# A decoder layer in split fp32: one weight block of the down projection's seven products comes by accumulating transfers alone, product 1 moves one quad forward, and the second pass takes a fourth quad in sevens

## The chip, the cores and the metric

The kernel runs on one core of a Trainium2 chip. The metric is the device time of one execution in microseconds. A trace of one profiled execution of the kernel before is at hand; times in it count from the start of the span.

## The reference

One decoder layer on 256 tokens of 2048 channels, all in fp32: a half-step SwiGLU feed-forward block, a mixer of two attention branches, and a second half-step feed-forward block, each with a residual and a layer norm. What the change touches is the last matrix product of the two feed-forward blocks, from 5632 hidden channels to 2048:

```python
def _swiglu(x, w_gate, w_up, w_down):
    return (jax.nn.silu(x @ w_gate) * (x @ w_up)) @ w_down
...
h = _layer_norm(ALPHA * h + 0.5 * _swiglu(h, ffn1_w_gate[l], ffn1_w_up[l], ffn1_w_down[l]),
                ln1_g[l], ln1_b[l])
```

## The kernel before

**Three matmuls for one.** fp32 precision is kept by splitting each operand into a rounded high part and a remainder (`split`, L154 and L155): ScalarE casts the block, VectorE subtracts the cast from it. A product of two split operands is then three matmuls, high by high, high by low, low by high (`triple`, L208 to L210). So every weight block of 128 x 1024 elements costs a cast on ScalarE and a subtraction on VectorE before TensorE can use it. The split blocks, named `wring`, stand in a ring of six pairs. A pair comes free when TensorE has used it.

**Units.** The work of a matrix product is cut into units. `unit` (L194) issues a unit's load at once, splits the weights of the unit that was loaded three units ago, and issues the matmuls of one that was prepared four units ago. So the order in which units are called sets the order on every engine, with these distances between load, split and matmuls. A list of functions due at a unit (`calls`) adds the loads of h, their splits and the like.

**The down projection.** It runs in two passes p, each over two column blocks m of 512 columns; each unit takes 256 of the 5632 rows. Four 128-row tiles of h make a quad, 11 of them. A *plain* unit multiplies one weight block with both halves b of the tokens: 2 tiles x 2 halves x 3, so 12 matmuls; a quad has four plain units per pass. A quad can also be taken *in sevens* (Strassen's scheme in Winograd's form): its four weight blocks 11, 12, 21, 22 (row pair, then column block) are combined into seven sums, each split and multiplied with one of seven forms of h, at 2 x 3 matmuls a product. The forms are made by `QuadForms.steps` from the raw h: four differences (L569) and seven split pieces, written to tiles named `xs`. Three quads, 0 to 2, go in sevens in both passes; their forms are made once, in the first pass, and kept.

**The seven products' weights** (`Sliced`, from L583). Product 1 takes block 11 as it is, 5 takes 11 + 12, 6 takes 11 + 12 + 22, 7 takes 12 + 22, 2 takes 21, 4 takes 11 + 12 + 22 + 21 and 3 takes 22; they come in the order 1, 5, 6, 7, 2, 4, 3. The sums are made in place in three buffers named `sraw`, one each for 11, 12 and 22, loaded by SyncE (L656); 21 comes into a tile of the plain units' pool `raw` of four buffers (L652). VectorE adds 12 to 11 for product 5, 22 to that for 6, 21 to that for 4 (L661). For product 7, 12 + 22 is an accumulating transfer: GpSimd issues a transfer of 22 from DRAM that is added onto the buffer of 12 (L663); only in the very first quad of the first pass VectorE adds it. A buffer is loaded anew when its last reader is done.

**Order of units.** A string, `mix`, says where a product (s) and where a plain unit (p) stands; the rest of the plain units follows. After the products' sums are complete, VectorE folds them into the residual rows `z` (L863), and after the last plain unit of a column block it adds that block and takes statistics (L880, L889). In the first feed-forward block, tables for the attention (`setup`, masks, angles) are made on VectorE and ScalarE about where the two passes meet. The h of a quad comes back from DRAM by transfers on GpSimd's queue (`get_h`, L990), called six units before its first use.

Of the kernel before, what the change touches and what calls it, by code (L numbers as in the profile page):

```python
# [11 lines left out]
F32 = mybir.dt.float32  # L12
# [47 lines left out]
def layer_kernel(ctx: ExitStack, tc: tile.TileContext, a: dict, out: bass.AP):  # L60
    nc = tc.nc
    V, S, GP, PE = nc.vector, nc.scalar, nc.gpsimd, nc.tensor
# [90 lines left out]
    def split(hi, lo, src):  # L153
        cast[0] = S.copy(hi, src)  # L154
        lows[0] = V.tensor_tensor(out=lo, in0=src, in1=hi.bitcast(F32), op=ALU.subtract)  # L155
        return lows[0]
# [426 lines left out]
    class Sliced:  # L583
# [2 lines left out]

        def __init__(self, at):
            self.at = at
            self.R = {n: act_tile([P, 1024], F32, "sraw") for n in ("11", "12", "22")}
            self.reads = {n: 0 for n in self.R}  # L590

        def run(self, w0, w1, units, forms, fold, done, calls, tail=0):

            R = self.R
            plan = {1: ("11", "11", None, "A"), 5: ("12", "11", "12", "D"), 6: ("22", "11", "22", "B"),
                    7: (None, "12", "22", "C"), 2: ("21", "21", None, (0, 0)), 4: (None, "11", "21", (0, 1)),
                    3: (None, "22", None, (1, 0))}
            uses = {"11": 4, "12": 2, "22": 3}
            banks, seen, shared = {}, {}, {}
            keys = [(n, b) for n in range(2) for b in range(2)]  # L600
            total = {key: 2 * sum(1 for u in units if len(u) == 2 and u[0] == key[0]) for key in keys}
# [36 lines left out]
            held = {}  # L638

            def product(q, p):  # L640
                load_block, src, other, key = plan[p]
                st = {}

                def by_transfer(q):
                    return tail > 0 or q > 0

                def load():
                    w = (w0, w1)[load_block[1] == "2"]
                    j = 2 * q + (load_block[0] == "2")
                    if load_block == "21":  # L650
                        held["21"] = wpool.tile([P, 1024], F32, tag="raw", name=nm("raw"), bufs=4)
                        nc.sync.dma_start(held["21"], w[j])  # L652
                    else:
                        assert self.reads[load_block] == 0, (q, p, self.reads)
                        self.reads[load_block] = uses[load_block]
                        nc.sync.dma_start(R[load_block], w[j])  # L656

                def prep():
                    t = held["21"] if src == "21" else R[src]
                    if other is not None and not (p == 7 and by_transfer(q)):  # L660
                        V.tensor_tensor(out=t, in0=t, in1=held["21"] if other == "21" else R[other], op=ALU.add)  # L661
                    if p == 5 and by_transfer(q):
                        nc.gpsimd.dma_start(R["12"], w1[2 * q + 1], accum_op=ALU.add)  # L663
                    for name in (src, other):
                        if name in R:
                            self.reads[name] -= 1
# [277 lines left out]
    def ffn(n, x, wgu, wdn, residual, g, bt, each, first=None, between=None, nxt=None, cols=None, norm=None, pending=None):  # L944
# [111 lines left out]
        spare = []  # L1056
        forms = {q: QuadForms(spare) for q in range(3)}
        down = Sliced(h_at)
        order = (1, 5, 6, 7, 2, 4, 3)

        def quad_units(quads):
            return [(m, 2 * q + i) for q in quads for m in range(2) for i in range(2)]

        for p in range(2):
            if p == 0:
                rest = deque(quad_units(range(3, KF // 4)))
                mix = "pppp" + "spspspspspspspppp" * 2 + "sp" * 7
                kept = ()
            else:
                kept = (9, 10)  # L1070
                rest = deque(quad_units((9, 10, 3, 4)) + [(m, 2 * q + i) for m in range(2) for q in (5, 6, 7, 8) for i in range(2)])
# [9 lines left out]
            for q in range(3, KF // 4):  # L1081
# [5 lines left out]
            if p == 0:  # L1087
                for q in range(3):
                    first_use = units.index((q, 1, None))
                    if q > 0:  # L1090
# [4 lines left out]
            else:  # L1095
# [528 lines left out]
```

## Time and profile before

| what | value |
|---|---|
| median of 3 runs | 1960.17 us (1960.05 to 1962.89) |
| the profiled execution's own time | 1958.59 us |
| its span, first to last instruction | 1956.8 us |
| TensorE, VectorE, ScalarE, GpSimd busy | 99%, 90%, 65%, 19% of the span |
| granted TensorE clock | 0.999 |
| down projection of the first block: first pass, mixed part of the second | 449 to 565 us, 565 to 660 us |
| the same of the second block | 1715 to 1830 us, 1830 to 1924 us |

The profile says for each engine how long it was busy, and for each idle time what ended it. An engine that is busy all the time still need not be the bound of a stretch: matmuls overlap, so a pitch, the distance of their starts, says more than a length. Idle time matters only on the engine that bounds. For the others it is a reserve, and the list of waits says what it is made of: waits for the bounding engine cost nothing, waits for a transfer may.

### The profile page before, as it was taken

What the parts mean: (1) busy time and instruction counts of PE and PEld (TensorE: products, weight loads), DVE (VectorE), ACT (ScalarE), POOL (GpSimd) and SP (SyncE); (2) the same over time, 40 slices, a digit from 0 to 9 for tenths busy, and PEclk for the clock granted to TensorE, in tenths of its full rate; (3) what the DMA queues carried; (4) which work ended last, traced back from release to release, by engine and by line L of the source; (5) the groups of instructions that cost most, each with busy time, mean ns of one, the idle gap of its engine ahead of it and who ended that gap; (6) DMA issues with size and microseconds to landing.
All of it is one profiled execution on the core that took longest, in us unless ns stands there. A gap on an engine that the chain in (4) does not pass through costs nothing.

```text
span 1956.8 us, 25750 instructions
## 1 busy us (share of the span) xinstructions
PE 1943.6 (99%) x8715; PEld 1608.7 (82%) x8715; DVE 1760.2 (90%) x2129; ACT 1277.6 (65%) x1638; POOL 376.1 (19%) x610
## 2 busy tenths in 40 slices
PE   9999999999999999999999999999999999999998
PEld 8888888888888898888888888888888888888886
DVE  7999999999898879989987777789999999999987
ACT  6677676776665566666667655566767676766652
POOL 0122212321200010102241630012221123210110
PEclk9999999999999999999999999999999999999999
DMA  9988997888878667767685798698989888888973
GB/s 319 304 241 244 269 304 238 237 267 289 291 239 258 208 221 255 238 220 257 211 256 190 234 301 279 202 294 251 251 255 283 280 232 245 272 305 259 314 246 127
DMA packets 152245, 498.30 MB, mean 255 GB/s; under 512 B 22017, under 2 KB 22321, under 8 KB 152113
## 3 DMA queue, kind: packets, MB, share of 16 engines
q1 hardware_dynamic: 110592, 371.64, 53.2%
q0 software_dynamic: 41376, 124.89, 27.1%
q8 instruction: 68, 1.11, 0.2%
q14 instruction: 65, 0.52, 0.1%
q10 hardware_dynamic: 144, 0.13, 0.0%
HBM read 466.16 MB, written 30.41 MB: 254 GB/s over the span
## 4 chain that ended last, share of the span: by engine, by line
PE 91%; DVE 5%; DMA 2%; issue 2%; ACT 0%; POOL 0%; SPq 0%; DVEq 0%; ACTq 0%
PE mm L209 25%; PE mm L208 25%; PE mm L210 25%; PE tr L209 4%; PE tr L210 4%; PE tr L208 4%; DVE wring L155 3%; DMA raw<-in_gu_dram 1%; DVE sraw L452 1%; PE tr L715 0%; DMA raw<-in_dn_dram 0%; DMA raw<-in_wgd_dram 0%; PE tr L1425 0%; PE tr L1427 0%; ACT wring L154 0%
## 5 line engine op out<-in xcount | busy, mean ns | idle before, releaser
L154 ACT CAST wring<-sraw 128x1024 fp32r<-128x1024 f32 (+1 forms) x576 | 567.5, 1009 | 182.0 <-DVE sraw L452 61.2
L155 DVE TENSOR_TENSOR wring<-sraw,wring 128x1024 fp32r<-128x1024 f32 (+1 forms) x576 | 651.5, 1167 | 23.4 <-ACT wring L154 20.9
L154 ACT CAST wring<-raw 128x1024 fp32r<-128x1024 f32 (+2 forms) x436 | 448.0, 1033 | 277.0 <-PE mm L210 187.5
L155 DVE TENSOR_TENSOR wring<-raw,wring 128x1024 fp32r<-128x1024 f32 (+2 forms) x436 | 518.8, 1198 | 101.2 <-ACT wring L154 98.7
L208 PE MATMUL mm<-wring,h 128*128 128x512 f32 (+2 forms) x1152 | 443.7, 385 | 0.1
L210 PE MATMUL mm<-wring,h 128*128 128x512 f32 (+2 forms) x1152 | 443.0, 385 | 0.0
L209 PE MATMUL mm<-wring,h 128*128 128x512 f32 (+2 forms) x1152 | 442.6, 384 | 0.0
L210 PEld LDWEIGHTS mm<-wring,h 128*128 128x128 f32 x1152 | 216.4, 188 | 43.2 <-DVE h L155 0.7
L208 PEld LDWEIGHTS mm<-wring,h 128*128 128x128 f32 x1152 | 216.4, 188 | 43.1 <-ACT h L154 0.6
L209 PEld LDWEIGHTS mm<-wring,h 128*128 128x128 f32 x1152 | 216.4, 188 | 42.2
L209 PE MATMUL mm<-wring,xs 128*128 128x512 f32 x616 | 240.2, 390 | 0.6 <-DVE wring L155 0.5
L210 PE MATMUL mm<-wring,xs 128*128 128x512 f32 x616 | 239.7, 389 | 0.0
L208 PE MATMUL mm<-wring,xs 128*128 128x512 f32 x616 | 239.6, 389 | 0.0
L452 DVE TENSOR_TENSOR sraw<-sraw,sraw 128x1024 f32<-128x1024 f32 x168 | 191.7, 1168 | 1.2 <-DMA sraw<-in_wdk_dram 1.1
L761 POOL DMA_DIRECT2D hT<-blocks x176 | 97.2, 559 | 212.1 <-DVE blocks L759 108.7
L209 PEld LDWEIGHTS mm<-wring,xs 128*128 128x128 f32 x616 | 115.6, 188 | 26.5 <-DVE wring L155 2.7
L208 PEld LDWEIGHTS mm<-wring,xs 128*128 128x128 f32 x616 | 115.6, 188 | 24.0
L210 PEld LDWEIGHTS mm<-wring,xs 128*128 128x128 f32 x616 | 115.6, 188 | 23.9
L454 POOL DMA_DIRECT2D sraw<-in_gu_dram x60 | 52.4, 917 | 383.5 <-DVE sraw L452 356.8
L209 PE MATMUL mm<-wring,x 128*128 128x512 f32 x240 | 93.8, 391 | 0.5 <-DVE wring L155 0.5
L210 PE MATMUL mm<-wring,x 128*128 128x512 f32 x240 | 93.4, 389 | 0.0
L208 PE MATMUL mm<-wring,x 128*128 128x512 f32 x240 | 92.6, 390 | 0.3 <-ACT wring L154 0.3
(345 smaller groups left out, 2686.3 us busy)
## 6 DMA issues: line engine op xcount, KB each, us to landing
sraw<-in_gu_dram SPq DMA_DIRECT2D x156, 512.0 KB, 7.3
raw<-in_dn_dram SPq DMA_DIRECT2D x140, 512.0 KB, 4.8
raw<-in_gu_dram SPq DMA_DIRECT2D x110, 512.0 KB, 7.3
sraw<-in_gu_dram POOLq DMA_DIRECT2D x104, 512.0 KB, 7.6
sraw<-in_dn_dram SPq DMA_DIRECT2D x36, 512.0 KB, 5.7
raw<-in_w_out_dram SPq DMA_DIRECT2D x32, 512.0 KB, 4.3
hraw<-hT POOLq DMA_DIRECT2D x56, 256.0 KB, 6.1
raw<-in_wgd_dram SPq DMA_DIRECT2D x24, 512.0 KB, 4.4
```

The source lines that it names most:

```text
L154: cast[0] = S.copy(hi, src)
L155: lows[0] = V.tensor_tensor(out=lo, in0=src, in1=hi.bitcast(F32), op=ALU.subtract)
L208: PE.matmul(o, xh, wh, start=first, stop=False, skip_group_check=again)
L209: PE.matmul(o, xh, wl, start=False, stop=False, skip_group_check=again)
L210: PE.matmul(o, xl, wh, start=False, stop=last, skip_group_check=again)
L452: last = V.tensor_tensor(out=stored(src, i), in0=stored(src, i), in1=stored(add[1], i), op=ALU.add)
L454: nc.gpsimd.dma_start(stored("22", s), source("12", s), accum_op=ALU.add)
L761: nc.gpsimd.dma_start(to.rearrange("(g r) (i f) -> i r g f", g=4, i=4)[i], t[32 * i:32 * (i + 1), :].rearrange("r (g f) -> r g f", g=4))
```

## The change

Buffer 12 is gone; the three `sraw` buffers are now two for 11, used by quads in turn, and one for 22. Block 12 is never loaded by itself: after product 1 has been split, GpSimd issues a transfer that adds 12 onto the buffer of 11 (L671 of the new program), and after VectorE has added 22 to 11 for product 6, another adds 12 onto the buffer of 22 (L667). Product 5 then splits 11 + 12 and product 7 splits 12 + 22 with no addition of VectorE; 6 and 4 keep theirs. The order is 1 of the first quad, then for each quad 3, 5, 6, then 1 of the next quad, then 2, 7, 4. The second pass takes quad 3 in sevens too; its forms are made there. Both strings are new. The transfers of a pass change with this: per feed-forward block SyncE issues 7 loads fewer and GpSimd 9 accumulations more.

```diff
-            self.R = {n: act_tile([P, 1024], F32, "sraw") for n in ("11", "12", "22")}
+            self.R = {n: act_tile([P, 1024], F32, "sraw") for n in (("11", 0), ("11", 1), ("22", 0))}
...
-            plan = {1: ("11", "11", None, "A"), 5: ("12", "11", "12", "D"), 6: ("22", "11", "22", "B"),
-                    7: (None, "12", "22", "C"), 2: ("21", "21", None, (0, 0)), 4: (None, "11", "21", (0, 1)),
-                    3: (None, "22", None, (1, 0))}
-            uses = {"11": 4, "12": 2, "22": 3}
+            plan = {1: ("11", "11", None, "A"), 5: (None, "11", None, "D"), 6: (None, "11", "22", "B"),
+                    7: (None, "22", None, "C"), 2: ("21", "21", None, (0, 0)), 4: (None, "11", "21", (0, 1)),
+                    3: ("22", "22", None, (1, 0))}
+            uses = {"11": 4, "22": 3}
...
-                def by_transfer(q):
-                    return tail > 0 or q > 0
+                def stored(name):
+                    return name, q % 2 if name == "11" else 0
...
                 def prep():
-                    t = held["21"] if src == "21" else R[src]
-                    if other is not None and not (p == 7 and by_transfer(q)):
-                        V.tensor_tensor(out=t, in0=t, in1=held["21"] if other == "21" else R[other], op=ALU.add)
-                    if p == 5 and by_transfer(q):
-                        nc.gpsimd.dma_start(R["12"], w1[2 * q + 1], accum_op=ALU.add)
+                    t = held["21"] if src == "21" else R[stored(src)]
+                    if other is not None:
+                        V.tensor_tensor(out=t, in0=t, in1=held["21"] if other == "21" else R[stored(other)], op=ALU.add)
...
+                    if p == 6:
+                        nc.gpsimd.dma_start(R[stored("22")], w1[2 * q], accum_op=ALU.add)
                     pair = next_pair()
                     split(*pair, t)
+                    if p == 1:
+                        nc.gpsimd.dma_start(t, w1[2 * q], accum_op=ALU.add)
...
-        order = (1, 5, 6, 7, 2, 4, 3)
+        def products_of(n):
+
+            yield 0, 1, None
+            for q in range(n):
+                for f in (3, 5, 6):
+                    yield q, f, None
+                if q + 1 < n:
+                    yield q + 1, 1, None
+                for f in (2, 7, 4):
+                    yield q, f, None
...
-                mix = "pppp" + "spspspspspspspppp" * 2 + "sp" * 7
+                mix = 'ppppppspppspspspspspspspspspspspspspspspspspspspsp'
...
-                mix = "p" + "spspspspspspsppp" * 2 + "spspspspspss"
-            products = deque((q, f, None) for q in range(3) for f in order)
+                mix = 'pspppssspspsspspssspspsspspssspspsspspssspppssps'
+            products = deque(products_of(sevens))
```

Two places show it. The first is VectorE in the second pass of the second feed-forward block. Before, `sraw_1846`, `sraw_1847` and `sraw_1848` are the buffers of 11, 12 and 22; here a quad's products 5, 6 and 7 are made, among the additions and statistics of the first pass (`z`, `bn`):

```order
L661 TENSOR_TENSOR sraw_1846_13624<-sraw_1846_13624,sraw_1847_13625 128x1024
L155 TENSOR_TENSOR h_1984_14733<-hraw_1969_14645,h_1983_14732 128x512 x2
L880 SCALAR_TENSOR_TENSOR z_1882_13841<-mm_1877_13785,z_1882_13841 128x512
L155 TENSOR_TENSOR wring_542_5029<-sraw_1846_13624,wring_541_5028 128x1024
L880 SCALAR_TENSOR_TENSOR z_1888_13864<-mm_1878_13792,z_1888_13864 128x512
L155 TENSOR_TENSOR wring_15_115<-raw_1958_14564,wring_14_114 128x1024
L889 BN_STATS bn_1844_13622<-z_1882_13841 128x6
L889 BN_STATS bn_1845_13623<-z_1888_13864 128x6
L661 TENSOR_TENSOR sraw_1846_13624<-sraw_1846_13624,sraw_1848_13626 128x1024
L155 TENSOR_TENSOR wring_1453_10080<-raw_1959_14591,wring_1452_10079 128x1024
L155 TENSOR_TENSOR wring_1451_10078<-sraw_1847_13625,wring_1450_10077 128x1024
L155 TENSOR_TENSOR wring_1455_10082<-sraw_1846_13624,wring_1454_10081 128x1024
```

Now `sraw_1846` and `sraw_1847` are the two buffers of 11 and `sraw_1848` is that of 22; this is the fourth quad of the same pass, product 4 of the quad in front (`raw_2005` is its 21), then 3, 5 and 6:

```order
L662 TENSOR_TENSOR sraw_1846_13631<-sraw_1846_13631,raw_2005_14995 128x1024
L866 SCALAR_TENSOR_TENSOR z_1963_14613<-mm_1967_14637,z_1963_14613 128x512
L155 TENSOR_TENSOR wring_1451_10085<-raw_2012_15058,wring_1450_10084 128x1024
L155 TENSOR_TENSOR wring_1453_10087<-sraw_1846_13631,wring_1452_10086 128x1024
L155 TENSOR_TENSOR h_2017_15114<-hraw_2009_15034,h_2016_15113 128x512
L155 TENSOR_TENSOR h_2021_15146<-hraw_2011_15055,h_2020_15145 128x512 x2
L155 TENSOR_TENSOR wring_1449_10083<-sraw_1848_13633,wring_1448_10082 128x1024
L155 TENSOR_TENSOR wring_542_5030<-sraw_1847_13632,wring_541_5029 128x1024
L843 MEMSET gbraw_2025_15181 64x1024
L662 TENSOR_TENSOR sraw_1847_13632<-sraw_1847_13632,sraw_1848_13633 128x1024
L155 TENSOR_TENSOR wring_1455_10089<-raw_2018_15119,wring_1454_10088 128x1024
```

The addition ahead of product 5 is gone; the split of 22 for product 3 now stands ahead of 5, and three products follow one another with no plain unit between.

The second place is GpSimd's queue in the same pass. Before, accumulations onto 12 (`sraw_1847`) stand singly among the loads of h (`hraw`) and of the layer norm's gains (`gb`):

```order
L663 DMA sraw_1847_13625<-in_dn2_dram 128x1024
L990 DMA hraw_1986_14754<-hT2_10361 128x512
L990 DMA hraw_1993_14876<-hT2_10361 128x512 x2
L990 DMA hraw_1996_14906<-hT2_10361 128x512 x2
L990 DMA hraw_2005_14967<-hT2_10361 128x512 x2
L990 DMA hraw_2011_15031<-hT2_10361 128x512 x2
L663 DMA sraw_1847_13625<-in_dn2_dram 128x1024
```

Now the accumulations onto 22 (L667) and onto 11 (L671) come in turn, with loads of h and of gains behind them:

```order
L667 DMA sraw_1848_13633<-in_dn2_dram 128x1024
L671 DMA sraw_1847_13632<-in_dn2_dram 128x1024
L667 DMA sraw_1848_13633<-in_dn2_dram 128x1024
L671 DMA sraw_1846_13631<-in_dn2_dram 128x1024
L993 DMA hraw_2009_15034<-hT2_10368 128x512 x2
L993 DMA hraw_2011_15055<-hT2_10368 128x512 x2
L833 DMA gb_2014_15109<-in_ln3_g_dram 128x1024
L667 DMA sraw_1848_13633<-in_dn2_dram 128x1024
```

Each accumulation waits for an instruction of VectorE, the addition for product 6 or the split of product 1, and what is queued behind it on GpSimd waits too.

More of the change, by code (lines that the diff above doesn't have):

```diff
@@ L1055, in ffn @@
             later(84, setup)
-        spare = []
-        forms = {q: QuadForms(spare) for q in range(3)}
+        spare, made = [], set()
+        forms = {q: QuadForms(spare) for q in range(4)}
         down = Sliced(h_at)
-        order = (1, 5, 6, 7, 2, 4, 3)
+        def products_of(n):
[7 more added lines that the diff above has]
+                    yield q, f, None
         def quad_units(quads):
@@ L1065, in ffn @@
             if p == 0:
-                rest = deque(quad_units(range(3, KF // 4)))
-                mix = "pppp" + "spspspspspspspppp" * 2 + "sp" * 7
+                sevens = 3
+                rest = deque(quad_units(range(sevens, KF // 4)))
+                mix = 'ppppppspppspspspspspspspspspspspspspspspspspspspsp'
                 kept = ()
             else:
+                sevens = 4
                 kept = (9, 10)
-                rest = deque(quad_units((9, 10, 3, 4)) + [(m, 2 * q + i) for m in range(2) for q in (5, 6, 7, 8) for i in range(2)])
-                mix = "p" + "spspspspspspsppp" * 2 + "spspspspspss"
-            products = deque((q, f, None) for q in range(3) for f in order)
+                rest = deque(quad_units((9, 10, *range(sevens, 5))) + [(m, 2 * q + i) for m in range(2) for q in (5, 6, 7, 8) for i in range(2)])
+                mix = 'pspppssspspsspspssspspsspspssspspsspspssspppssps'
+            products = deque(products_of(sevens))
             units = [(products if c == "s" else rest).popleft() for c in mix]
@@ L1080, in call @@
                 calls.setdefault(max(i, 0), []).append(fn)
-            for q in range(3, KF // 4):
+            for q in range(sevens, KF // 4):
                 first_use = min(i for i, u in enumerate(units) if len(u) == 2 and u[1] // 2 == q)
@@ L1086, in ffn @@
                 call(first_use, lambda q=q: split_h(q))
-            if p == 0:
-                for q in range(3):
+            for q in range(sevens):
+                if q not in made:
+                    made.add(q)
                     first_use = units.index((q, 1, None))
-                    if q > 0:
+                    if (p, q) != (0, 0):
                         call(first_use - 6, lambda q=q: get_h(q))
@@ L1094, in ffn @@
                     call(first_use + 3, lambda q=q: got.pop(q))
-            else:
+            if p == 1:
                 call(len(units) - 8, widen)
```

11 lines of the change are left out of this document (6 added, 5 removed).

## The prediction

> **What bounds the kernel now.** I read the page's head first, then the list of what TensorE waited for over the whole span, then busy time in the stretches of the two feed-forward blocks' down projections, which are all that the change touches. The four rows of the windows are the first pass of the first block, the mixed part of its second pass, and the same two of the second block. Their columns are the stretch, its length, then the busy us of PE, PEld, DVE, ACT and POOL, the granted clock, the share of the DMA engines and GB/s.
>
> ```profile
> span 1956.8 us, 25750 instructions
> PE 1943.6 (99%) x8715; PEld 1608.7 (82%) x8715; DVE 1760.2 (90%) x2129; ACT 1277.6 (65%) x1638; POOL 376.1 (19%) x610
> ```
> ```profile
> PE tr L911 <- ACT pair L909: 4.1, 1, 4.1
> PE tr L98 <- DVE zero L96: 1.1, 1, 1.1
> PE mm L209 <- DVE wring L155: 1.0, 4, 0.3
> PE tr L209 <- DVE wring L155: 0.9, 1, 0.9
> ```
> ```profile
> 449.00:565.00 116.00, 116.00 (x514) 96.04 (x513) 104.58 (x133) 73.63 (x92) 20.09 (x36) 1.00 0.82 283
> 565.00:660.00 95.00, 94.10 (x416) 77.57 (x415) 86.22 (x107) 57.09 (x61) 5.35 (x8) 1.00 0.75 232
> 1715.00:1830.00 115.00, 115.00 (x509) 95.23 (x508) 108.02 (x129) 70.62 (x90) 14.84 (x27) 1.00 0.85 285
> 1830.00:1924.00 94.00, 94.00 (x417) 77.83 (x416) 83.75 (x90) 57.38 (x65) 10.41 (x19) 1.00 0.80 261
> ```
>
> TensorE is the bound: in three of the four stretches it has no gap, and in the fourth, 95.00 less 94.10, it has one of 0.9 us. VectorE runs at 89 to 94% behind it. So two things can move the time: the number of matmuls, and whether VectorE still delivers each split weight block in time. The one gap is this, on TensorE's timeline (start, length, and the idle time before it with its releaser):
>
> ```profile
> 575.78 0.39 PE L208 MATMUL tr<-wring,xs 128*128 128x512 f32 x1
> 577.07 0.50 PE L209 MATMUL tr<-wring,xs 128*128 128x512 f32 x1 [0.90 <-DVE wring L155]
> ```
>
> The product's first matmul, on the cast half, could go; the second needs the remainder, which VectorE had not yet written.
>
> **Fewer matmuls.** A product of two blocks of 128 rows is six matmuls; a plain unit, both token halves, is twelve. The pitch is read where a plain unit is followed by a product:
>
> ```profile
> 1899.74 0.39 PE L208 MATMUL mm<-wring,h 128*128 128x512 f32 x1
> ...
> 1901.10 0.39 PE L208 MATMUL mm<-wring,xs 128*128 128x512 f32 x1
> ...
> 1902.46 0.39 PE L208 MATMUL mm<-wring,h 128*128 128x512 f32 x1
> ```
>
> Six matmuls from 1901.10 to 1902.46 are 1.36 us, 0.227 us each (the 0.39 is one matmul's own length, which overlaps the next). The fourth quad of the second pass goes from four plain units, 48 matmuls, to seven products, 42. Two blocks: 12 matmuls fewer, which is also what the order of the two programs counts, 8543 rows against 8531. That is 12 x 0.227 = **2.72 us less**. By the Trainium skill (page "TensorE: Matmul & The Clock Gate", section "Back-to-back issue gap") a stream of weight loads and 512-column matmuls sustains about 131 ns each. By that figure the twelve would be worth an estimated 1.6 us; the trace differs, with 227 ns, and decides.
>
> **VectorE's work.** Its pitch is shorter than the length of an instruction, because neighbours overlap: the pair below starts at 555.88 and the next instruction at 558.15, so 1.14 us for 1024 columns. Smaller pieces are costed at their means; the last row is ScalarE's cast.
>
> ```profile
> 555.88 2.35 DVE L155 TENSOR_TENSOR wring<-raw,wring 128x1024 fp32r<-128x1024 f32 x2
> 558.15 1.02 DVE L1137 SCALAR_TENSOR_TENSOR bias<-dist,mask 128x384 f32<-128x384 f32 x2
> ```
> ```profile
> L569 DVE TENSOR_TENSOR f<-hraw 128x256 f32<-128x256 f32 x6 | 2.4, 419 | 0.0
> L155 DVE TENSOR_TENSOR xs<-hraw,xs 128x256 fp32r<-128x256 f32 x9 | 3.6, 418 | 0.0
> L155 DVE TENSOR_TENSOR xs<-f,xs 128x512 fp32r<-128x512 f32 x6 | 4.0, 686 | 0.7 <-ACT xs L154 0.7
> L155 DVE TENSOR_TENSOR h<-hraw,h 128x512 fp32r<-128x512 f32 x14 | 9.3, 684 | 0.0
> L154 ACT CAST wring<-raw 128x1024 fp32r<-128x1024 f32 x39 | 40.3, 1049 | 16.8 <-PE mm L210 10.6 <-DVE wring L155 3.9 <-DMA raw<-in_dn_dram 1.4
> ```
>
> First pass, each block: additions fall from 10 to 6, since products 5 and 7 need none: 4 x 1.14 = 4.6 us less. Second pass: additions fall from 9 to 8 (-1.1); three more weight splits, seven instead of four for the new quad (+3.4); and its seven forms of h, four differences and three splits of 256 columns more than the two plain splits of 512 (7 x 0.42 = +2.9). Together **+5.2 us**, while TensorE's mixed part falls to 28 x 1.36 + 20 x 2.72 = 92.5 us. So VectorE would be busy 86.2 + 5.2 = 91.4 us of 92.5 in the first block and 83.75 + 5.2 = 88.95 in the second. What stays idle is 1.1 and 3.6 us, where it was 8.8 and 10.2. ScalarE gains 3 x 1.05 + 3 x 0.4 = 4.4 us on 57 and has room.
>
> What did VectorE wait for in these idle times? First its own waits in the two second passes, then ScalarE's, first block and second:
>
> ```profile
> DVE wring L155 <- ACT wring L154: 8.0, 10, 1.5
> ```
> ```profile
> DVE wring L155 <- ACT wring L154: 8.2, 12, 1.5
> ```
> ```profile
> ACT wring L154 <- PE mm L210: 19.5, 16, 1.7
> ACT wring L154 <- DMA raw<-in_dn_dram: 6.0, 5, 1.4
> ...
> ACT wring L154 <- DMA sraw<-in_dn_dram: 3.5, 2, 2.5
> ```
> ```profile
> ACT wring L154 <- PE mm L210: 15.6, 13, 1.7
> ACT wring L154 <- DMA raw<-in_dn_dram: 8.4, 5, 2.9
> ...
> ACT h L154 <- DMA hraw<-hT: 3.9, 1, 3.9
> ```
>
> For the cast, that is for TensorE (the ring of six was full: harmless) and for transfers: 6.0 + 3.5 = 9.5 us and 8.4 + 3.9 = 12.3 us. If these transfer waits stay and all reach VectorE, its lack is 9.5 - 1.1 = 8.4 and 12.3 - 3.6 = 8.7 us. Against it stands the ring's reserve: five units in front of TensorE, 5 x 92.5/48 = 9.6 us, less a cast and a split (1.05 + 1.14), 7.4 us. What is left over is 1.0 + 1.3 = **2.3 us** of new gaps. Bounds: 0, when half the waits stay hidden as they are now; 17.1, when the reserve is spent before. I take 2.3: full waits against a full reserve, both ends being extreme. The old gap of **0.9 us** goes: the addition for product 5 ahead of it is gone and the first pass leaves VectorE 4.6 us more.
>
> **The transfers.** Each block has 9 accumulating transfers more on GpSimd's queue (14 instead of 5) and 7 loads fewer on SyncE's. The rows are lengths of such an issue, the landings in the second pass of the second block, and the queues' shares of the DMA engines:
>
> ```profile
> L663 POOL DMA_DIRECT2D sraw<-in_dn_dram x10: 871/888/908, 491.5 to 1893.2; - x10
> ...
> DMA to landing us min/median/max: 3.1/5.0/9.6
> ```
> ```profile
> sraw<-in_dn_dram SPq DMA_DIRECT2D x6, 512.0 KB, 6.2
> ...
> sraw<-in_dn_dram POOLq DMA_DIRECT2D x2, 512.0 KB, 5.6
> ```
> ```profile
> q1 hardware_dynamic: 110592, 371.64, 53.2%
> q0 software_dynamic: 41376, 124.89, 27.1%
> ```
>
> Per MB of the span, queue q0 takes 0.271 x 1957/124.9 = 4.2 us of the engines and q1 2.8. A second pass gets 5 accumulations and loses 4 loads of 0.52 MB: 11.1 - 5.9 = +5.3 us in 92.5, so 0.80 becomes about 0.86: not full. Block 22 is the tight buffer, since 12 is added to it after product 6 and the next quad's 22 overwrites it after product 7. From 6 to 7 lie five units, 9.5 us of TensorE; landing, cast and split take 5.6 + 1.05 + 1.14 = 7.8, so 1.7 us spare. From 7 to the next quad's 3 lie four units, 8.2 us; 6.2 + 2.2 = 8.4, short by 0.2. The accumulation onto 11 has 10.9 us or more. I cost these at nothing; the ring covers them. On GpSimd an accumulation waits for VectorE's addition or split, and the loads of h stand behind it: they are called six units early, about 11.6 us, against 0.89 of issue and a landing like those above.
>
> **Sum**, against the profiled execution's own 1958.59 us (1.8 us outside its span): -2.7 - 0.9 + 2.3 = -1.3 us. The median shown is 1960.17, 1.6 us above that execution; the difference carries over, so **1958.8 us**.
>
> **Rivals.**
> A, everything stays covered: no new gap, 1960.17 - 3.6 = 1956.5 us. For it: three of four stretches have no gap though waits of this size are in them. Against: VectorE never had as little as 1.1 us idle there.
>
> B, slower: VectorE becomes the bound of both second passes. Its mechanism is the sum above with an empty ring: the reserve is used up by the evacuations and additions that come in a heap where the passes meet, and each transfer wait becomes a gap of TensorE. Up to 17.1 - 3.6 = +13.5 us, 1973.7; with half the reserve, 2.3 + 7.4 = 9.7 of gaps, 1966.2. It turns slower than before by over 3.9 us when the two reserves together give under 9.6 us of their 14.8. For it: the gap at 577 is of this kind, at a VectorE share of 91%, where now 96 and 99% are due.
>
> C, late accumulations: if they landed at 9.6 us, the longest row, instead of 5.6, each would overrun its spare 1.7 by 2.3 us, eight times in the two second passes' quads; with nothing idle that is 18 us, and less the reserve of one pass 11: 1967. By the Trainium skill (page "SBUF — State Buffer", section "SBUF: two separate sides") a transfer issued by GpSimd can starve for descriptors while VectorE runs an instruction in a two-port mode. The trace does not show that here: 5.6 us against 6.2 for SyncE's loads, with VectorE at 89%.
>
> That the change does not save its matmuls is excluded by the order.
>
> **How the numbers follow.** 0.2% is 3.9 us, about what a measurement of this kernel can tell from no change; the runs before spread over 2.8 us. My forecast has 0.52, A 0.22, B 0.19, C 0.07. A lies just inside the bound, so a third of it, 0.07, counts as faster. B and C, but for their mild ends, are slower: 0.22. The rest, 0.71, is the same. The range goes from 1956.0, A with half a us of spread, to 1964.8, gaps of 8.3 us, between my sum and half the reserve; beyond it lies most of B and C.
>
> **What would show it.** In the profile after, the pitch of 0.227 us stands, and TensorE's waits in the down stretches are all on VectorE's splits, some 2 us, in the second passes; VectorE is busy over 95% there; no gap at 577. It is wrong if the first passes show gaps, if TensorE waits more than 5 us, or if accumulations land far later than 6 us.

## The result, and the profile after

| | median | runs |
|---|---|---|
| before | 1960.78 us | 1960.05 to 1962.89, 4 runs |
| after | 1983.13 us | 1980.80 to 1983.31, 4 runs |

The ratio is 1.0109, 95% interval 1.0092 to 1.0127: the change costs 22 us, where 1958.8 us was forecast. The profiled execution took 1980.8 us, 1.8 of them outside its span. The ratios here and below are not those of the two medians, so the two can differ by up to 0.07%.

The head of the page, and TensorE's waits over the whole span:

```profile
span 1979.0 us, 25787 instructions
PE 1950.2 (99%) x8703; PEld 1607.7 (81%) x8703; DVE 1758.0 (89%) x2139; ACT 1281.4 (65%) x1650; POOL 391.9 (20%) x628
```
```profile
PE mm L209 <- DVE wring L155: 6.6, 13, 0.8
PE tr L914 <- ACT pair L912: 4.1, 1, 4.1
PE mm L208 <- ACT wring L154: 2.9, 3, 1.5
PE tr L718 <- DVE z L940: 2.4, 1, 2.4
PE tr L208 <- ACT wring L154: 2.4, 2, 1.5
```

The 12 matmuls are gone (8715 to 8703). New are waits not only for the remainder (L209 on VectorE) but for the cast itself (L208 on ScalarE): the step ahead of VectorE was late. The same four stretches as before, and the end of the second block's mixed part, say where:

```profile
449.00:565.00 116.00, 112.03 (x483) 90.75 (x483) 96.86 (x138) 71.31 (x93) 24.36 (x41) 0.99 0.84 275
565.00:660.00 95.00, 95.00 (x421) 78.69 (x420) 83.31 (x97) 58.09 (x66) 9.03 (x12) 1.00 0.76 225
1715.00:1830.00 115.00, 114.77 (x505) 94.18 (x504) 103.45 (x126) 70.39 (x89) 15.10 (x24) 1.00 0.87 279
1830.00:1924.00 94.00, 88.92 (x378) 71.11 (x376) 73.91 (x84) 51.29 (x63) 14.71 (x24) 0.98 0.79 248
1924.00:1946.00 22.00, 18.00 (x74) 13.84 (x75) 18.55 (x22) 10.37 (x11) 3.36 (x6) 1.00 0.63 194
```

TensorE is idle for 4.0 us in the first block's first pass and for 5.1 + 4.0 us in the second block's second pass and its end. In the worst of them VectorE is busy for only 73.9 of 94 us: it is not the bound, it waits too. Idle time also understates the loss, as TensorE's timeline shows:

```profile
1892.76 0.39 PE L210 MATMUL mm<-wring,h 128*128 128x512 f32 x1
1894.62 0.49 PE L208 MATMUL mm<-wring,xs 128*128 128x512 f32 x1 [1.47 <-ACT wring L154]
1895.88 0.50 PE L209 MATMUL mm<-wring,xs 128*128 128x512 f32 x1 [0.77 <-DVE wring L155]
...
1900.51 0.49 PE L208 MATMUL tr<-wring,xs 128*128 128x512 f32 x1 [1.47 <-ACT wring L154]
1901.77 0.79 PE L209 MATMUL tr<-wring,xs 128*128 128x512 f32 x1 [0.77 <-DVE wring L155]
...
1902.79 0.63 PE L208 MATMUL tr<-wring,xs 128*128 128x512 f32 x1
1903.21 0.63 PE L209 MATMUL tr<-wring,xs 128*128 128x512 f32 x1
```

From 1892.76 to 1895.88 two matmuls start in 3.1 us instead of 0.45. After the last of these gaps the pitch is 0.42 us instead of 0.227 for a while. The stretch around them, in the kernel after and then in the kernel before:

```profile
1890.00:1906.00 16.00, 11.45 (x39) 7.95 (x39) 10.81 (x13) 9.62 (x13) 1.38 (x2) 0.89 0.65 212
```
```profile
1890.00:1906.00 16.00, 16.00 (x72) 13.27 (x71) 12.58 (x12) 9.09 (x11) 1.47 (x2) 1.00 0.69 208
```

39 matmuls run where the kernel before runs 72 in the same time: 33 x 0.227, some 7.5 us lost in this one place. Matched matmul by matmul with the trace of before, the kernel after is 7.0 us behind at the end of the first block's first pass, 4.4 us at the end of the mixed part of its second pass, 7.3 us at the first transpose of the rows `z` behind it (687.74 against 680.42, after the wait of 2.4 us for `z`), 8.8 us at the end of the second block's first pass, and 22.2 us at the end. So the first pass of the first block and the second pass of the second block, with its end, make nearly all of the loss.

**Back from the gap.** TensorE waits at 1894.62 for a cast of ScalarE, and that one waited 7.48 us for the load of block 22 for product 3. First ScalarE's timeline, then VectorE's split for product 7, SyncE's and GpSimd's issues around it, the landing of the load at 1881.01 alone, and what the DMA engines carried from 1876.7 to 1893.43:

```profile
1893.53 1.04 ACT L154 CAST wring<-sraw 128x1024 fp32r<-128x1024 f32 x1 [7.48 <-DMA sraw<-in_dn_dram]
```
```profile
1879.76 1.22 DVE L155 TENSOR_TENSOR wring<-sraw,wring 128x1024 fp32r<-128x1024 f32 x1
```
```profile
1881.01 0.35 SPq L657 DMA_DIRECT2D sraw<-in_dn_dram  x1
...
1884.62 0.33 SPq L657 DMA_DIRECT2D sraw<-in_dn_dram  x1
```
```profile
1876.73 0.84 POOL L671 DMA_DIRECT2D sraw<-in_dn_dram  x1 [2.92 <-DVE wring L155]
1877.27 2.49 POOL L993 DMA_DIRECT2D hraw<-hT  x4
1879.42 0.86 POOL L833 DMA_DIRECT2D gb<-in_ln_g_dram  x1
```
```profile
sraw<-in_dn_dram SPq DMA_DIRECT2D x1, 512.0 KB, 12.4
```
```profile
DMA packets 1676, 5.46 MB, mean 327 GB/s; under 512 B 217, under 2 KB 217, under 8 KB 1675
...
raw<-in_dn_dram SPq DMA_DIRECT2D x4, 512.0 KB, 11.3
hraw<-hT POOLq DMA_DIRECT2D x4, 256.0 KB, 12.0
sraw<-in_dn_dram SPq DMA_DIRECT2D x2, 512.0 KB, 12.2
sraw<-in_dn_dram POOLq DMA_DIRECT2D x1, 512.0 KB, 9.8
```
```profile
1876.73:1893.43 16.70, 16.42 (x73) 13.24 (x71) 10.88 (x15) 6.18 (x9) 3.56 (x6) 1.00 0.97 327
```

The load of 22 leaves at 1881.01, when product 7's split has released the buffer, and lands at 1893.4, after 12.4 us. It is issued into a burst: the accumulation of 12 onto 11, four loads of h, a gain vector, four blocks for the `raw` tiles and the next 11, with the DMA engines busy for 97% of 16.7 us. In between they idle: the share over the whole stretch is only 0.79.

### The profile page after: what moved, and what is told of

The parts are those of the page before. It is cut to its first block, busy times and chain, and to the rows that moved or that the text cites. A ratio compares the mean times of both kernels' runs of the same rounds, so it can differ in the third digit from the quotient of the medians.

```text
span 1979.0 us, 25787 instructions
## 1 busy us (share of the span) xinstructions
PE 1950.2 (99%) x8703; PEld 1607.7 (81%) x8703; DVE 1758.0 (89%) x2139; ACT 1281.4 (65%) x1650; POOL 391.9 (20%) x628
## 4 chain that ended last, share of the span: by engine, by line
PE 45%; DVE 10%; DMA 9%; issue 4%; ACT 2%; POOL 0%; DVEq 0%; ACTq 0%; POOLq 0%
PE mm L209 13%; PE mm L208 13%; PE mm L210 13%; DVE wring L155 6%; DMA sraw<-in_dn_dram 4%; PE tr L209 1%; PE tr L210 1%; PE tr L208 1%; ACT wring L154 1%; DMA raw<-in_dn_dram 1%; DVE sraw L452 1%; DMA pt<-pturn 1%; DVE sraw L662 1%; DMA hT<-blocks 1%; PE tr L718 0%
## 5 line engine op out<-in xcount | busy, mean ns | idle before, releaser
L154 ACT CAST wring<-sraw 128x1024 fp32r<-128x1024 f32 (+1 forms) x588 | 579.6, 1010 | 242.5 <-PE mm L210 69.1
L155 DVE TENSOR_TENSOR wring<-sraw,wring 128x1024 fp32r<-128x1024 f32 (+1 forms) x588 | 664.8, 1164 | 51.6 <-ACT wring L154 50.2
L155 DVE TENSOR_TENSOR wring<-raw,wring 128x1024 fp32r<-128x1024 f32 (+2 forms) x430 | 509.5, 1195 | 98.0 <-ACT wring L154 96.1
L154 ACT CAST wring<-raw 128x1024 fp32r<-128x1024 f32 (+2 forms) x430 | 441.1, 1032 | 234.0 <-PE mm L210 142.1
L209 PE MATMUL mm<-wring,h 128*128 128x512 f32 (+2 forms) x1120 | 431.5, 385 | 3.4 <-DVE wring L155 3.2
L208 PE MATMUL mm<-wring,h 128*128 128x512 f32 (+2 forms) x1120 | 431.8, 386 | 0.1
L210 PE MATMUL mm<-wring,h 128*128 128x512 f32 (+2 forms) x1120 | 430.7, 385 | 0.0
L209 PE MATMUL mm<-wring,xs 128*128 128x512 f32 x632 | 247.4, 391 | 2.8 <-DVE wring L155 2.8
L209 PEld LDWEIGHTS mm<-wring,h 128*128 128x128 f32 x1120 | 210.6, 188 | 48.6 <-DVE wring L155 8.0
L208 PE MATMUL mm<-wring,xs 128*128 128x512 f32 x632 | 246.3, 390 | 2.9 <-ACT wring L154 2.9
L210 PE MATMUL mm<-wring,xs 128*128 128x512 f32 x632 | 246.5, 390 | 0.0
L208 PEld LDWEIGHTS mm<-wring,h 128*128 128x128 f32 x1120 | 210.7, 188 | 42.3 <-ACT h L154 0.6
L210 PEld LDWEIGHTS mm<-wring,h 128*128 128x128 f32 x1120 | 210.5, 188 | 41.6 <-DVE h L155 0.7
L209 PEld LDWEIGHTS mm<-wring,xs 128*128 128x128 f32 x632 | 118.9, 188 | 30.2 <-DVE wring L155 5.8
L208 PEld LDWEIGHTS mm<-wring,xs 128*128 128x128 f32 x632 | 118.8, 188 | 28.6 <-ACT wring L154 4.1
L210 PEld LDWEIGHTS mm<-wring,xs 128*128 128x128 f32 x632 | 118.9, 188 | 24.4
L209 PE MATMUL tr<-wring,xs 128*128 128x512 f32 x244 | 96.0, 394 | 2.8 <-DVE pair L845 1.8
L208 PE MATMUL tr<-wring,xs 128*128 128x512 f32 x244 | 95.4, 391 | 2.4 <-ACT wring L154 2.4
L210 PE MATMUL tr<-wring,xs 128*128 128x512 f32 x244 | 95.4, 391 | 0.0
```

The costliest lines, as they stand in the source:

```text
L208: PE.matmul(o, xh, wh, start=first, stop=False, skip_group_check=again)
L209: PE.matmul(o, xh, wl, start=False, stop=False, skip_group_check=again)
L210: PE.matmul(o, xl, wh, start=False, stop=last, skip_group_check=again)
```

## The experiments

Three theories stood at first. **L**: the loop through the one buffer of 22 is as long as TensorE's work for a quad. **Q**: GpSimd's queue holds loads of h and gains behind an accumulation that waits for VectorE, and lets them go in a heap. **V**: VectorE has too much work. Each kernel starts from the changed one unless its edit says otherwise.

### Two buffers for 22

```diff
-            self.R = {n: act_tile([P, 1024], F32, "sraw") for n in (("11", 0), ("11", 1), ("22", 0))}
+            self.R = {n: act_tile([P, 1024], F32, "sraw") for n in (("11", 0), ("11", 1), ("22", 0), ("22", 1))}
...
-                    return name, q % 2 if name == "11" else 0
+                    return name, q % 2
```


> The changed kernel with two buffers for block 22, used by quads in turn as those of 11 are. The load of the next quad's 22 then no longer waits for product 7 of the quad in front. Theory L (the loop through the one buffer of 22: load, cast and split for 3, addition for 6, accumulation of 12, cast and split for 7, next load; two turns in the trace took 20.7 and 28.8 us where TensorE has some 20 us of work for a quad): most of the 24 us of new gaps go, 1960 to 1968 us. Theory Q (GpSimd's queue holds loads of h and gains behind accumulations and lets them go in a heap, which slows the load of 22): the heaps stay and the load stays slow, 1973 to 1981 us. Theory V (VectorE has too much work with the fourth quad): unchanged, 1980 to 1983 us.

Measured: 1961.78 us beside 1961.12 us of before, ratio 1.0001 (0.9991 to 1.0012). The loss is gone, but nothing is gained. The third quad's 22 now left at 1852.67, ahead of the burst, and landed after 5.9 us. In the burst stands the load of the last quad's 22: SyncE's timeline, the landing of that load alone, and ScalarE's cast of it.

```profile
1870.43 0.33 SPq L657 DMA_DIRECT2D sraw<-in_dn_dram  x1
```
```profile
sraw<-in_dn_dram SPq DMA_DIRECT2D x1, 512.0 KB, 12.4
```
```profile
1898.52 1.03 ACT L154 CAST wring<-sraw 128x1024 fp32r<-128x1024 f32 x1
```

It takes 12.4 us, as long as the one that made the gap, but it leaves 28 us ahead of its cast, as soon as the quad two before it has released that buffer, and the cast waits for nothing. So this long landing costs nothing, because the load leaves early. V is out too: VectorE's work is the same here, and the loss is gone.

### One of the two accumulations left out

Without the one onto 22 (L667), then without the one onto 11 (L671):

```diff
-                        nc.gpsimd.dma_start(R[stored("22")], w1[2 * q], accum_op=ALU.add)
+                        pass
```


> The changed kernel without the accumulation of 12 onto 22 (product 7 then uses 22 alone, so the result is not the reference's); VectorE's work is the same. Theory L: one landing of 6 to 7 us leaves the loop of 22, which falls to 14 to 22 us, under TensorE's 20 in most turns: 1960 to 1967 us. Theory Q: half of the accumulations leave GpSimd's queue, those onto 11 still hold h and gains back; half of the loss goes, 1969 to 1975 us. Theory V: 1980 to 1983 us.

```diff
-                    if p == 1:
-                        nc.gpsimd.dma_start(t, w1[2 * q], accum_op=ALU.add)
```


> The changed kernel without the accumulation of 12 onto 11 (product 5 then uses 11 alone, and 6 and 4 lack 12, so the result is not the reference's); the same seven transfers fewer per pair of passes as are left out for the other one, VectorE's work is the same. Theory L: the loop of 22 is as it was, 1976 to 1983 us. Theory Q: as for the other one, 1969 to 1975 us, since half of the accumulations leave the queue. Theory V: 1980 to 1983 us.

Measured: 1974.67 us, ratio 1.0075 (1.0060 to 1.0090), without the one onto 22; 1960.62 us, ratio 1.0001 (0.9992 to 1.0010), without the one onto 11. Both are far from what L and V expected; Q has the first but not the second, since it expected them alike. L falls in this form: with one landing out of the loop, the loads of 22 still left 20.5 us apart (1857.81, 1878.29), where seven products and four plain units, TensorE's work between them, are 7 x 1.36 + 4 x 2.72 = 20.4. The same number of the same transfers is worth 8 us in the one place and 22 in the other. What differs is what they stand beside: the one onto 11 leaves 4 us ahead of the load of 22, the one onto 22 lands before that load leaves. ScalarE's cast of the same load of 22, in the one and the other:

```profile
1890.23 1.04 ACT L154 CAST wring<-sraw 128x1024 fp32r<-128x1024 f32 x1 [6.90 <-DMA sraw<-in_dn_dram]
```
```profile
1877.83 1.05 ACT L154 CAST wring<-sraw 128x1024 fp32r<-128x1024 f32 x1 [3.97 <-DMA sraw<-in_dn_dram]
```

### Three quads in the second pass

```diff
-                sevens = 4
+                sevens = 3
...
-                mix = 'pspppssspspsspspssspspsspspssspspsspspssspppssps'
+                mix = "p" + "spspspspspspsppp" * 2 + "spspspspspss"
```


> The changed kernel with three quads in sevens in the second pass, as before the change, with the string of units of before there; the new buffers, accumulations and product order stay in both passes. Theory L: in the second passes a quad now has 16 units, some 29 us, for a loop of 20 to 29, so most of the gaps there go; those of the first pass of the first block (6.6 us) stay, 12 matmuls more: 1967 to 1972 us. Theory Q: the accumulations still hold the queue, 1970 to 1976 us. Theory V: VectorE has its old work or less, 1958 to 1961 us.

Measured: 1959.43 us, ratio 0.9998 (0.9989 to 1.0008). Only V has this number, and V is out by the runs above, in which VectorE's work stayed and the loss went. The gaps of the second passes went, as L expected; but so did those of the first pass, which has the same units:

```profile
449.00:565.00 116.00, 116.00 (x513) 95.80 (x512) 103.04 (x148) 78.49 (x102) 24.38 (x41) 1.00 0.87 290
```

There the load of 22 that leaves at 522.07 takes 8.6 us; in the changed kernel its twin, at 520.80, takes 12.8. GpSimd's issues around it differ: four loads of h at once 0.7 us behind the load in the changed kernel, two of them 8 us behind it here and the other two later still. First the changed kernel, then this one:

```profile
521.53 2.13 POOL L993 DMA_DIRECT2D hraw<-hT  x4 [3.00 <-PE mm L210]
```
```profile
530.14 1.07 POOL L993 DMA_DIRECT2D hraw<-hT  x2 [10.35 <-DVE h L155]
```

So what travels beside the load seems to count. That can be the wait in GpSimd's queue (Q), or the transfers' own weight. The next runs part them.

### The wait without the bytes, the bytes without the wait

```diff
-                        nc.gpsimd.dma_start(t, w1[2 * q], accum_op=ALU.add)
+                        nc.gpsimd.dma_start(t[:, :8], w1[2 * q][:, :8], accum_op=ALU.add)
```


> The changed kernel with the accumulation onto 11 cut to 8 of its 1024 columns: GpSimd still waits for the split of product 1 before it, and the loads of h and of gains behind it wait too, but its 0.5 MB are gone (product 5, 6 and 4 lack most of 12, so the result is not the reference's). Theory Q (the wait holds back loads of h and gains, which then leave in a heap just ahead of the loads of the next 22 and 11, which land after 12 instead of 5 to 6 us): the heap stays, 1975 to 1982 us. Theory B (the bytes of the added transfers fill the DMA engines when 22 is loaded): as without the transfer, 1960 to 1963 us. Theory L (the one buffer of 22 alone): 1976 to 1983 us.

```diff
+            self.spare = act_tile([P, 1024], F32, "sraw")
...
-                        nc.gpsimd.dma_start(t, w1[2 * q], accum_op=ALU.add)
+                        nc.gpsimd.dma_start(self.spare, w1[2 * q])
```


> The opposite: the transfer of 12 keeps its size and its place in GpSimd's queue but goes into a buffer of its own that nobody reads, without adding, so that it doesn't wait for VectorE (product 5, 6 and 4 lack 12, so the result is not the reference's). Theory Q: the h and gain loads go out when asked for, 1960 to 1965 us. Theory B: the bytes are the same, 1975 to 1983 us. Theory L: 1976 to 1983 us.

Measured: 1963.15 us, ratio 1.0022 (1.0010 to 1.0034), with the wait alone, 4.4 us above the before of its runs (1958.72) where the changed kernel was 22 above; 1977.56 us, ratio 1.0090 (1.0073 to 1.0107), with the bytes alone. Q, which expected 1975 us or more of the first, falls as the main cause: the wait is still there and most of the loss is not. B, the weight of the bytes, expected 1960 to 1963 us. The second run is weaker than it looks: with no split to wait for, the transfers left earlier than meant, each waited for the one before it in the one spare buffer, and loads of h stood behind them:

```profile
497.22 0.53 POOL L672 DMA_DIRECT2D sraw<-in_dn_dram  x1 [6.33 <-DMA sraw<-in_dn_dram]
504.93 0.53 POOL L672 DMA_DIRECT2D sraw<-in_dn_dram  x1 [7.18 <-DMA sraw<-in_dn_dram]
505.45 2.14 POOL L994 DMA_DIRECT2D hraw<-hT  x4
```

TensorE then stood idle for 5.5 us in one gap ahead of 511.61. So that run has a wait of its own making, and it decides nothing.

### The loads of h on SyncE

```diff
-                nc.gpsimd.dma_start(raw[:, b, :], hT[q, b])
+                nc.sync.dma_start(raw[:, b, :], hT[q, b])
```


> The changed kernel with the loads of h for the down projections issued by SyncE instead of GpSimd; accumulations, waits and bytes stay, and the gains stay behind them on GpSimd. Theory Q: most of the loss goes, 1960 to 1967 us. Theory B and theory L: 1976 to 1983 us.

> Both cures together: two buffers for 22, and the loads of h issued by SyncE. If the long landing and the late issue of 22 are each half of the cause, what is left is the 12 matmuls saved and a few gaps: 1956 to 1960 us. If two buffers already took away all that the queue does: 1960 to 1962 us, as with two buffers alone. If SyncE's queue now holds weights behind h that wait for a buffer: over 1963 us.

Measured: 1975.92 us, ratio 1.0088 (1.0071 to 1.0105), and with two buffers for 22 besides 1972.95 us, ratio 1.0071 (1.0052 to 1.0090). The load of 22 of the third quad took 9.8 instead of 12.4 us, yet most of the loss stayed, against what Q expected. With two buffers the edit even costs some 14 us: 14.2 above the before of its runs, where the two buffers alone are 0.7 above theirs. Loads of h in SyncE's queue do harm; whether by weights that stand behind them was not tried apart. In the profiled execution with one buffer (1979.86 us, the longest of its four) some 6 us of the loss arise between 1100 and 1150, in the attention, with a wait of 3.4 us for a transfer of `pt`. What that has to do with the edit is not shown.

### The same transfer without the addition

```diff
-                        nc.gpsimd.dma_start(t, w1[2 * q], accum_op=ALU.add)
+                        nc.gpsimd.dma_start(t, w1[2 * q])
```


> The changed kernel with the transfer of 12 onto 11 as a plain one: same queue, same place, same wait for the split of product 1, same 0.5 MB, but it overwrites instead of adding (product 5 then uses 12 alone, 6 and 4 lack 11, so the result is not the reference's). Theory A (an accumulating transfer holds the DMA engines twice as long per byte: in the trace of before one of 0.52 MB took 53.9% of 5.8 us, 3.1 us of all engines, where plain loads of 2.96 MB took 95.2% of 9 us, 1.5 us for 0.52 MB): some 1.6 us of engine time less for each of the seven of a block, the long landings shrink, 1962 to 1969 us. Theory B (the bytes, whatever the form): as the changed kernel, 1974 to 1983 us.

Measured: 1969.58 us, ratio 1.0049 (1.0033 to 1.0064): 8 us above before, so some 12 of the 22 us (by the ratios) to 14 (by the medians) go with the addition alone, at the same place, wait and bytes. The time is half a us above what A expected and 4 us below what B did. The price could be read before the change. The rows are of the kernel before: the queues from 1859.8 to 1865.6, with one accumulating transfer, and from 1875 to 1884, with plain loads (packets, MB, share of the 16 engines).

```profile
q0 software_dynamic: 144, 0.52, 53.9%
```
```profile
q1 hardware_dynamic: 853, 2.96, 95.2%
```

53.9% of 5.8 us is 3.1 us of all engines for 0.52 MB; 95.2% of 9 us is 8.6 us for 2.96 MB, so 1.5 us for 0.52 MB. These two rows differ in the queue as well as in the addition. The runs part the two: GpSimd's queue over the whole span, first without the transfers onto 11 (span 1961.2 us), then with the fourteen as plain ones (1965.1), then with them as accumulations (1979.0):

```profile
q0 software_dynamic: 41952, 126.99, 27.7%
```
```profile
q0 software_dynamic: 43968, 134.33, 28.7%
```
```profile
q0 software_dynamic: 43968, 134.33, 29.5%
```

That is 543, 564 and 584 us of all engines. A plain transfer on this queue takes 21/14 = 1.5 us, an accumulating one 41/14 = 2.9 us. So it is the addition, not the queue, that doubles what a transfer takes from the others here. A full stretch alone is not new: the 95.2% above are from the kernel before, and TensorE has no gap there.

In seven runs with four quads in sevens the third quad's load of 22 leaves on the buffer's release. The cast's wait is the landing less 4.9 to 5.8 us, whatever made the landing long:

| kernel | landing of 22, us | the cast's wait, us | ratio to before |
|---|---|---|---|
| changed | 12.4 | 7.48 | 1.0109 |
| without onto 22 | 11.8 | 6.90 | 1.0075 |
| onto 11 without addition | 11.3 | 6.35 | 1.0049 |
| onto 11 cut to 8 columns | 10.2 | 4.47 | 1.0022 |
| h on SyncE | 9.8 | 4.89 | 1.0088 |
| without onto 11 | 9.7 | 3.97 | 1.0001 |
| onto a spare buffer | 9.7 | 3.90 | 1.0090 |

This is one load of one profiled execution, the ratio is the whole time. Five of the seven times follow the order. h on SyncE and the spare buffer do not; the latter loses 10 us in the first pass of the first block, where the wait of its own making stands.

### The fourth quad alone

The kernel before, its buffers, accumulations and product order kept, with the fourth quad of the second pass in sevens:

```diff
+                sevens = 4
...
-                mix = "p" + "spspspspspspsppp" * 2 + "spspspspspss"
+                mix = 'p' + ('spspspsssspp' * 4)[:-1]
```


> The kernel before with only the fourth quad of the second pass in sevens: its own three buffers, accumulations (one per quad) and product order, units strung as four times s p s p s p s s s s p p. Theory A or B (the added accumulations make the loss): nothing is added but one accumulation per block, so 1956 to 1961 us. Theory V (the second pass has no room on VectorE: its additions are 12 instead of 8 here, 4.6 us more than in the changed kernel, 93 to 96 us of work in 92.5 us of TensorE): gaps in both second passes, 1963 to 1972 us.

Measured: 1968.54 us, ratio 1.0036 (1.0024 to 1.0048), the number that V expected. But VectorE is not full, as V had it: it is busy for 86.3 of 95 and 85.7 of 94 us in the second passes. ScalarE's waits in the first block's second pass:

```profile
ACT wring L154 <- DVE sraw L661: 22.7, 11, 3.8
ACT wring L154 <- DMA sraw<-in_dn_dram: 7.7, 3, 3.8
```

The casts wait for VectorE's additions, and for a third of that time for loads into `sraw`. So the fourth quad probably needs fewer additions in front of its casts, and the accumulations take one of a quad's three away; the two waits were not run apart. What the accumulations ask for in return is the DMA engines.

### A version that beats both

First the loads of h earlier, on top of two buffers for 22:

```diff
-                call(first_use - 6, lambda q=q: get_h(q))
+                call(first_use - 9, lambda q=q: get_h(q))
```


> Two buffers for 22, and the loads of h for the down projections called nine units ahead of their use instead of six. Some of them then leave before the accumulations of the second pass and no longer with the loads of 22 and 11. If the bytes around the load of 22 are what is left of the loss: 1955 to 1959 us. If what is left is VectorE, which in two22 is busy without a break for 20 us ahead of its gap of 1.7 us: 1960 to 1963 us. If the earlier loads of h only collide with others: over 1963 us.

Measured: 1962.40 us, ratio 1.0009 (1.0000 to 1.0017), no better than two buffers alone. TensorE's idle time from 1830 to 1924 went from 2.1 us with two buffers alone to none; the first pass of the first block lost part of that again (113.79 us busy of 116, where with two buffers alone it was 115.13). Hence the loads of h earlier in the second passes only, and two plain units more in the last quad, where with two buffers alone VectorE ran without a break for some 20 us ahead of a gap of TensorE of 1.6 us.

```diff
-                call(first_use - 6, lambda q=q: get_h(q))
+                call(first_use - (6, 9)[p], lambda q=q: get_h(q))
...
-                mix = 'pspppssspspsspspssspspsspspssspspsspspssspppssps'
+                mix = 'pspppssspspsspspssspspsspspssspspsspspspsspppsspps'
```


> Two buffers for 22; the loads of h nine units ahead in the second passes only (in the first passes that made 22's first loads land after 10 us); and in the last quad two plain units more, one between products 3 and 5 and one between 7 and 4, where VectorE was busy without a break. If the gaps left in two22 (1.4 us in the first pass, some 3 in the second pass of the second block, 2 to 3 at its end) are these two things: 1956 to 1959 us. If the last quad's chain of addition for 6, accumulation and split for 7 sets the end whatever stands between: 1960 to 1962 us.

Measured: **1956.37 us** beside 1960.12, ratio 0.9983 (0.9974 to 0.9991). TensorE's waits, and the two second passes:

```profile
PE tr L914 <- ACT pair L912: 4.1, 1, 4.1
PE tr L98 <- DVE zero L96: 1.1, 1, 1.1
PE mm L209 <- DVE wring L155: 0.8, 3, 0.3
```
```profile
565.00:660.00 95.00, 95.00 (x421) 78.67 (x420) 84.68 (x91) 58.35 (x64) 8.26 (x11) 1.00 0.79 235
1830.00:1924.00 94.00, 94.00 (x415) 77.40 (x414) 88.33 (x100) 60.25 (x72) 13.08 (x20) 1.00 0.83 257
```

No wait of over 0.3 us is left in the down projections. The gain of 3.75 us (3.3 by the ratio, 1.8 to 5.1 by its interval) fits the 12 matmuls and the old gap, 2.7 + 0.9. Which of its two edits beside the second buffer did how much was not run apart.

## Why the prediction was wrong

- **12 matmuls, -2.7, and the old gap, -0.9**: right. The counts are 8715 and 8703, no gap stands at 577, and the last kernel gains about their sum.
- **"I cost these at nothing; the ring covers them"** is the step that failed, twice over. First the size: the accumulation was priced by its queue's mean, 4.2 us per MB, a mixture with plain loads of h; by its own row it is 6.0, and the same arithmetic gives 5 x 3.1 - 4 x 1.5 = +9.5 us of the engines per second pass instead of +5.3. Second, and this is what made the loss, the kind of number: a share of 0.86 over the stretch was called not full. Over the stretch it was even less, 0.76 and 0.79, but it was 0.97 in the 16.7 us up to the landing of 22. The way from 7 to the next 3, "short by 0.2", was worked out with a landing of 6.2 us. With 12.4 it is 8.2 - 14.6 = -6.4, and the cast's wait was 7.5. The ring did not cover that: the gaps behind that one load cost some 7.5 us.
- **The first passes** were expected without a gap, because VectorE gains room there. The first block's has 4.0 us, the second's 0.2. The same cause is likely: a load of 22 that left at 520.80, when its buffer was released, took 12.8 us and so landed at 533.6, and the cast that TensorE waits for starts at 533.70. The profile puts this cast's wait down to a matmul that ends at the same moment.
- **VectorE's lack, +2.3**: not the mechanism. "Busy over 95%" was wrong: 83.3 of 95 and 73.9 of 94 us. Where nothing else is late, in the last kernel, VectorE has 84.7 of 95 and 88.3 of 94 us of work in these stretches (91.4 and 89.0 were expected in 92.5), and TensorE has no gap.
- **GpSimd's loads of h** were given "a landing like those above"; in the burst four of them landed after 12.0 us (median).
- **Rival C**, given 0.07, came nearest: late landings against short spares. It named the wrong transfer as the one that makes the gap. The accumulations onto 22 landed after 5.5 us in the median, 9.9 at most; seven casts waited for them, 18.3 us in all, and without them 8 us come back. But the gap itself comes with the plain load of 22 beside the accumulation onto 11. **Rival B** names a spent reserve, which is what TensorE saw, but what spent it was waiting, not work. **Rival A** is what the change gives once the buffer is doubled and the loads of h are placed: 1956.5 was its number.
- What stays open: why the first block's `z` is late by 2.4 us; how the loss divides, since the addition, the bytes and the wait of the transfer onto 11, taken away in turn, are worth 12 to 14, 4 to 5 and some 4 us, and yet leaving out the one onto 22 gives back 8 too; and the harm of h on SyncE.

## What to carry to other kernels

Price a transfer by its own kind, in a stretch of the trace where it is nearly alone, not by its queue's mean: an addition in flight cost twice a plain load here. Then ask of every buffer when its load may leave at the earliest and what else leaves within the same ten microseconds; here a load tied to a release had the burst's landing of 12.4 us, not the 6.2 us of such loads in the kernel before. Where such a load is late, try a second buffer first: here it took the landing off the path without making it shorter.

## What the runs showed of the hardware

Short gaps cost more than their length here, because the clock follows. The stretch after the gaps at 1900.51 and 1901.77 (granted clock third from the end):

```profile
1901.38:1904.79 3.41, 3.02 (x7) 2.44 (x8) 3.41 (x5) 3.41 (x7) 0.00 (x0) 0.50 0.95 175
```

Two gaps of 1.47 and 0.77 us, 6 us after two others like them, brought 3.41 us at half the clock, 7 matmuls in the time of 15, or some 1.8 us. The same stands from 536.05 to 539.46, behind gaps of 1.10 and 0.76 us (granted clock 0.50, 6 matmuls). A gap of this size need not bring it: with two buffers for 22 one of 1.58 us, ahead of 1908.09, did not (granted clock 1.00 from 1908 to 1916). The Trainium skill (page "TensorE: Matmul & The Clock Gate", section "Part 1: The HAM clock gate") tells of a half-rate state that is set by windows of about 3.4 us, and of a cold pitch of 426.7 ns for 512 columns; the trace agrees, with 3.41 us and some 0.43 us. The page has it after an idle window; here TensorE was busy for much of the time before.
